# Turning copies with VectorE squares and DMAs in a two-layer hybrid encoder

## Chip, cores, metric

The kernel runs on one core of a Trainium2 chip. The metric is the device time of one execution in microseconds (us); smaller is better.

## What is computed

Two layers run over 256 tokens of width 2048, float32 in and out. Of the reference this matters:

```python
h = rmsnorm(x, pre_norm_g[l])
proj = jnp.einsum('bsd,dn->bsn', h, w_in[l])
(qa, ka, va, qb, kb, vb, qc, kc, vc, za, zb, zc, gates) = jnp.split(proj, ...)
ya = neighbourhood_attention(qa, ka, va, rpb[l])      # 8 heads
yb = gqa_attention(qb_h, kb_h, vb)                    # 8 heads, 2 of k and v; normed and rotated
yc = dilated_mixture(qc, kc, vc)                      # 3 groups of 4 heads, one softmax
g = sigmoid(gates + b_gate[l])
merged = (ga * ((ya * silu(za)) @ w_branch_a[l]) + gb * ((yb * silu(zb)) @ w_branch_b[l])
          + gc * ((yc * silu(zc)) @ w_branch_c[l]))
x = x + rmsnorm(merged @ w_out[l], post_norm_g[l])
```

Attention needs queries and keys with the head's 128 columns on the partitions, and its probabilities with the keys on the partitions; the projections by `w_branch` and `w_out` need their input with the columns on the partitions. A projection leaves the tokens on the partitions. So every such tensor is transposed once.

## The kernel before

**Weights.** All weights stream through the core once. A block is 512 output columns; its rows come in chunks of 256 (512 KB). A layer has 35 blocks of 8 chunks by the input weights, four times three smaller blocks by the branch weights (4, 2 and 4 chunks) and four blocks of 8 chunks by the output weight: 352 chunks a layer, 704 in all. SyncE (SP) issues one DMA a chunk into a tile `raw` (`emit_raw`, line 155; the first two chunks come by two DMAs each, line 163, all others by line 165). ScalarE rounds `raw` to a high part `wh` (line 171), VectorE subtracts it for the low part `wl` (line 176). TensorE multiplies each chunk for both token tiles T of 128 tokens, 12 matmuls of 512 columns a chunk (`mm3`, lines 146 to 148).

**Order.** The order of each engine's instructions is written out by the loop at line 737. Before chunk i it emits the `raw` up to chunk i+6, `wh` up to i+3 and `wl` up to i+2 (`ahead`, line 179; further in a few blocks), then the chunk's matmuls, then one `slot()` (line 100). A slot takes up to two steps of finished blocks' evacuations, one step of every active filler, and starts one new filler: first from `light` (transposes of evacuated blocks, put there by `later`), else from `heavy` (attention heads), no more than one head in 2 slots for the branches A and B, one in 4 for C. Every engine works through its own instructions in order; SP's queue holds the weight loads and all other DMAs.

**Buffers.** All large tiles come from one pool of 47 buffers of 4 KB a partition (`U`, line 59), taken in the order in which they come free. A DMA or an engine that writes into a buffer waits until its last reader is through.

**Transposes.** Everything that must be turned goes through TensorE as a 128x128 transpose into PSUM (`tp`), four side by side, and is copied or split from there into a high and a low part (`split`, line 128):

- `tr_job` (line 280): evacuated q, k, z and the rotated q, k of branch B, one job per token tile; transposes on line 284.
- `head_job` (line 360, branches A and B): a head's two products of scores, softmax, `norm`, then four transposes of the probabilities (line 380), a split, two slots later the products `o` with the values.
- `job_c` (line 407): the same for C, eight transposes a head through `four_T` (line 140).
- `mt_job` (line 568): the merged branches, through `four_T`.
- `ht_psum` (line 247): the second layer's input, through `four_T`; this one stays.

The split that follows is one ScalarE and one VectorE instruction. A head starts two slots after the one before it and takes nine slots in all; the heads of branch B start when the last tile of their q block has been evacuated.

Of the kernel before, what the change touches and what calls it, by code (L numbers as in the profile page):

```python
# [28 lines left out]
LAG = 6  # L29


class Blk:
    """One 512-column block of a projection: K chunks of 256 rows, both token tiles."""
# [14 lines left out]
def trunk(ctx, tc, x, xT, wpack, wbr_a, wbr_b, wbr_c, wout, pre_g, qk_g, bgate, post_g, abias,  # L48
# [32 lines left out]
    # the engines wake while the first loads are under way  # L81
# [11 lines left out]
    def later(g, wait=0):  # L93
        """a filler for a following slot, once what it needs is under way"""
        light.append((flow["slot"] + wait, g))
# [26 lines left out]
    def rsqrt(v, n):  # L122
        """1/sqrt of a small positive f32 tile"""
        y = small.tile([P, n], F32, name="rs_y")
        nc.gpsimd.tensor_tensor(out=y, in0=v, in1=mhalf[:, :n], op=ALU.pow)
        return y

    def split(src, h, lo, scale=1.0):
        """src * scale -> h + lo, both exactly representable for the one-pass products."""
# [6 lines left out]
    def four_T(src):  # L136
        """Four [128,128] transposes side by side in one bank."""
        tp = aux.tile([P, 4, P], F32, name="tp", bufs=2)
        for j in range(4):
            nc.tensor.transpose(tp[:, j, :], src(j), ident)  # L140
        return tp

    def mm3(out_, lhs, rhs, first, last):
        """out_ += lhs.T @ rhs for (high, low) pairs: one-pass products"""
# [60 lines left out]
    prev = {}  # L205

    def layer(l):
# [6 lines left out]
        # -- the layer's input: hT = (x * gain) transposed, 1/rms kept apart --  # L214
# [24 lines left out]
        def ht_x(nb, js):  # L239
            """from the host's transposed layout of x"""  # L240
# [6 lines left out]
        def ht_psum(nb, T):  # L247
            """from the previous layer's output: residual, transposes"""
# [30 lines left out]
        # -- evacuations, per token tile --  # L279
        def tr_job(dst, tok, T, n=4):  # L280
            """token-major [tok, n x 128] -> dst[column, block, tokens of T]; a pair is split"""
            tp = aux.tile([P, 4, P], F32, name="tp", bufs=2)
            for j in range(n):
                nc.tensor.transpose(tp[:, j, :], tok[:, T, j * P:(j + 1) * P], ident)  # L284
            c = slice(T * P, (T + 1) * P)
            if isinstance(dst, tuple):
                split(tp[:, 0:n], dst[0][:, 0:n, c], dst[1][:, 0:n, c])
            else:
                nc.scalar.copy(dst[:, 0:n, c], tp[:, 0:n])
            yield  # L290

        def evac_qk(store, key, which, two):
            tok = {}

            def f(T, ps):
# [4 lines left out]
                later(tr_job(store[key], tok[0], T))  # L300
# [16 lines left out]
        def evac_z(key):  # L317
            tok = {}

            def f(T, ps):  # L320
# [6 lines left out]
                later(tr_job(SZ[key], tok[0], T), 1)  # L327
# [3 lines left out]
        # -- attention --  # L331
        def softmax(sc, p, n, w, f=None):
            """n x w logits a row: exp(f * (s - max)), and the sums"""
# [11 lines left out]
        def norm(p, sm, n, rsh):  # L345
            """rows divided by their sums, times the gate's factor of the token"""
# [13 lines left out]
        def head_job(zb, hh, q, k, v, bias=None, f=None):  # L360
            """one head over all 256 keys, both token tiles: q, k give (high, low) of [d, tokens],
            v those of [keys of a tile, d]"""
# [14 lines left out]
            tp = aux.tile([P, 2, 256], F32, name="tp", bufs=2)  # L377
            for T in range(2):
                for kk in range(2):
                    nc.tensor.transpose(tp[:, kk, T * P:(T + 1) * P], p[:, T, kk * P:(kk + 1) * P], ident)  # L380
            pp = U("pp", [2, 2, 256], FR)
            ph, pl = pp[:, 0], pp[:, 1]
            split(tp, ph, pl)
# [23 lines left out]
        def job_c(hh, dist):  # L407
            """one merged head: the three groups' keys under one softmax"""
# [24 lines left out]
            px = U("px", [2, 256])  # L433
            for T in range(2):
                c = slice(T * P, (T + 1) * P)
                tp = four_T(lambda j: ps_[T][:, 0, j * P:(j + 1) * P])
                split(tp[:, 0:2], ph[:, :, c], pl[:, :, c])
                nc.scalar.copy(px[:, :, c], tp[:, 2:4])
                yield
# [10 lines left out]
        # -- branch A: two units of four heads --  # L450
# [17 lines left out]
        # -- branch B --  # L468
# [10 lines left out]
        def rope(dst, ps, T, n, which):  # L479
            """dst = rotation of ps (n heads), the norm's gain in the tables; in two steps"""  # L480
# [15 lines left out]
        def head_norm(ps, T, n):  # L496
            """1/rms of each head (of the normalised input's projection)"""
# [8 lines left out]
        def evac_qb(u):  # L506
            tok = {}

            def f(T, ps):
# [7 lines left out]
                later(tr_job(QT["b", u], tok[0], T), 1)  # L517
                if T == 1:
                    for hh in range(4):
                        heavy.append((2, job_b(u, hh)))  # L520
            return f

        def evac_kvb(T, ps):
# [14 lines left out]
            later(tr_job(KT["b"], tok, T, n=2), 1)  # L538
# [7 lines left out]
        # -- gates and branch products --  # L546
        def merge(nb):
# [20 lines left out]
            def mt_job(T):  # L568
                if nb not in MT:
                    MT[nb] = pair("mT", [4, 256])  # L570
                h, lo = MT[nb]
                c = slice(T * P, (T + 1) * P)
                tp = four_T(lambda j: G[0][:, T, j * P:(j + 1) * P])
                split(tp, h[:, :, c], lo[:, :, c], scale=0.5)
                yield

            def evac_p(i):
                def f(T, ps):
# [3 lines left out]
                    if i == 1:  # L582
                        later(mt_job(T))
# [9 lines left out]
        # -- output projection, post norm, residual --  # L593
# [258 lines left out]
```

## Time and profile before

| | |
|---|---|
| time, median of 3 runs (lowest to highest) | 2075.34 us (2074.78 to 2075.48) |
| span of the profiled execution, first to last instruction | 2073.5 us |
| around the span, against the median | 1.8 us |
| TensorE matmuls busy | 2061.9 us, 99% |
| VectorE, ScalarE busy | 1163.2 us (56%), 951.4 us (46%) |
| bytes moved by DMA | 397.81 MB, 192 GB/s |

The three runs lie within 0.04%. Busy time of TensorE includes matmuls that overlap one another: of two neighbours the next starts before the one before has ended, so the step from start to start is what a matmul costs. Instructions that only issue a DMA are listed under SPq and are not counted as busy time.

### The profile page before, as it was taken

What the parts mean: (1) busy time and instruction counts of PE and PEld (TensorE: products, weight loads), DVE (VectorE), ACT (ScalarE), POOL (GpSimd) and SP (SyncE); (2) the same over time, 40 slices, a digit from 0 to 9 for tenths busy, and PEclk for the clock granted to TensorE, in tenths of its full rate; (3) what the DMA queues carried; (4) which work ended last, traced back from release to release, by engine and by line L of the source; (5) the groups of instructions that cost most, each with busy time, mean ns of one, the idle gap of its engine ahead of it and who ended that gap; (6) DMA issues with size and microseconds to landing.
All of it is one profiled execution on the core that took longest, in us unless ns stands there. A gap on an engine that the chain in (4) does not pass through costs nothing.

```text
span 2073.5 us, 24944 instructions
## 1 busy us (share of the span) xinstructions
PE 2061.9 (99%) x9634; PEld 1716.2 (83%) x9634; DVE 1163.2 (56%) x1445; ACT 951.4 (46%) x1370; POOL 23.2 (1%) x31
## 2 busy tenths in 40 slices
PE   9999999999999999999999999999999999999998
PEld 7888888888888888888888888888888888888886
DVE  6444466565776554645554445565657764646454
ACT  6443354444554434443564444454445543443332
POOL 0000000000000000000000000000000000000000
PEclk9999999999999999999999999999999999999999
DMA  9555455645546655667565554555454466656662
GB/s 373 190 173 187 153 173 179 213 156 185 168 163 208 203 198 188 203 228 259 174 228 171 188 183 142 182 176 200 164 187 163 168 213 200 197 191 208 228 241 71
DMA packets 115270, 397.81 MB, mean 192 GB/s; under 512 B 12752, under 2 KB 12880, under 8 KB 115152
## 3 DMA queue, kind: packets, MB, share of 16 engines
q1 hardware_dynamic: 115152, 396.23, 56.5%
q8 instruction: 75, 1.23, 0.2%
q14 instruction: 43, 0.35, 0.1%
HBM read 391.99 MB, written 4.19 MB: 191 GB/s over the span
## 4 chain that ended last, share of the span: by engine, by line
PE 99%; DMA 0%; ACT 0%; DVE 0%; SPq 0%; issue 0%; DVEq 0%; POOLq 0%; ACTq 0%
PE acc L148 31%; PE acc L146 31%; PE acc L147 31%; PE tp L284 1%; PE tp L140 1%; PE tp L380 1%; PE o L148 0%; PE sc L148 0%; PE o L147 0%; PE sc L147 0%; PE o L146 0%; PE sc L146 0%; DMA raw<-in_wpack_dram 0%; PE o L446 0%; PE sc L418 0%; DVE x L597 0%
## 5 line engine op out<-in xcount | busy, mean ns | idle before, releaser
L176 DVE TENSOR_TENSOR wl<-raw,wh 128x1024 fp32r<-128x1024 f32 (+1 forms) x706 | 831.7, 1217 | 172.1 <-ACT wh L171 169.3
L146 PE MATMUL acc<-wh,hTh 128*128 128x512 f32 x2240 | 886.3, 396 | 0.6 <-ACT wh L171 0.6
L147 PE MATMUL acc<-wl,hTh 128*128 128x512 f32 x2240 | 873.8, 390 | 0.8 <-DVE wl L176 0.8
L148 PE MATMUL acc<-wh,hTl 128*128 128x512 f32 x2240 | 873.8, 390 | 0.0
L171 ACT CAST wh<-raw 128x1024 fp32r<-128x1024 f32 (+1 forms) x706 | 699.3, 1043 | 40.0 <-DVE wl L176 12.9
L148 PEld LDWEIGHTS acc<-wh,hTl 128*128 128x128 f32 x2240 | 420.6, 188 | 89.0
L147 PEld LDWEIGHTS acc<-wl,hTh 128*128 128x128 f32 x2240 | 421.5, 188 | 84.9 <-DVE wl L176 2.6
L146 PEld LDWEIGHTS acc<-wh,hTh 128*128 128x128 f32 x2240 | 421.2, 188 | 83.3 <-ACT wh L171 1.6
L564 ACT ACTIVATE g<-g 128x512 f32<-128x512 f32 x48 | 30.4, 633 | 232.8 <-DVE g L563 232.8
L563 DVE SCALAR_TENSOR_TENSOR g<-acc,rsx,bg 128x512 f32<-128x512 f32 x48 | 35.9, 747 | 173.6 <-PE acc L148 173.6
L146 PE MATMUL acc<-wh,yTh 128*128 128x512 f32 x320 | 124.5, 389 | 0.0
L147 PE MATMUL acc<-wl,yTh 128*128 128x512 f32 x320 | 124.5, 389 | 0.0
L148 PE MATMUL acc<-wh,yTl 128*128 128x512 f32 x320 | 124.5, 389 | 0.0
L146 PE MATMUL acc<-wh,mTh 128*128 128x512 f32 x256 | 100.4, 392 | 0.0
L148 PE MATMUL acc<-wh,mTl 128*128 128x512 f32 x256 | 99.7, 390 | 0.0
L147 PE MATMUL acc<-wl,mTh 128*128 128x512 f32 x256 | 99.7, 389 | 0.0
L299 ACT ACTIVATE tok<-acc,rsx 128x512 f32<-128x512 f32 x40 | 27.6, 689 | 124.9 <-PE acc L148 124.9
L340 ACT ACTIVATE sp<-sp,nm 128x256 f32<-128x256 f32 (+1 forms) x48 | 27.6, 577 | 109.4 <-DVE nm L335 109.4
L579 DVE SCALAR_TENSOR_TENSOR g<-g,acc 128x512 f32<-128x512 f32 x48 | 32.8, 683 | 78.6 <-PE acc L148 78.6
L147 PEld LDWEIGHTS acc<-wl,yTh 128*128 128x128 f32 x320 | 60.1, 188 | 12.5
L146 PEld LDWEIGHTS acc<-wh,yTh 128*128 128x128 f32 x320 | 60.1, 188 | 12.5
L130 ACT ACTIVATE mTh<-tp 128x512 fp32r<-128x512 f32 x16 | 9.6, 598 | 132.4 <-PE tp L140 132.4
(116 smaller groups left out, 1172.2 us busy)
## 6 DMA issues: line engine op xcount, KB each, us to landing
raw<-in_wpack_dram SPq DMA_DIRECT2D x558, 512.0 KB, 3.5
raw<-in_wo_dram SPq DMA_DIRECT2D x64, 512.0 KB, 5.2
raw<-in_wa_dram SPq DMA_DIRECT2D x32, 512.0 KB, 3.3
raw<-in_wb_dram SPq DMA_DIRECT2D x32, 512.0 KB, 3.7
raw<-in_wc_dram SPq DMA_DIRECT2D x16, 512.0 KB, 3.8
bg<-in_bgate_dram SPq DMA_DIRECT2D x24, 256.0 KB, 3.8
x<-in_x_dram SPq DMA_DIRECT2D x8, 512.0 KB, 7.9
abias<-in_abias_dram SPq DMA_DIRECT2D x8, 512.0 KB, 4.2
```

Of the source, the lines that this page charges most:

```text
L140: nc.tensor.transpose(tp[:, j, :], src(j), ident)
L146: nc.tensor.matmul(out_, lhsT=lh, rhs=rh, start=first, stop=False)
L147: nc.tensor.matmul(out_, lhsT=lh, rhs=rl, start=False, stop=False)
L148: nc.tensor.matmul(out_, lhsT=ll, rhs=rh, start=False, stop=last)
L171: nc.scalar.copy(HI[i][:, k], RAW[i][:, k])
L176: nc.vector.tensor_tensor(out=LO[i][:, k], in0=RAW[i][:, k], in1=f32(HI[i][:, k]), op=ALU.subtract)
L284: nc.tensor.transpose(tp[:, j, :], tok[:, T, j * P:(j + 1) * P], ident)
L299: nc.scalar.activation(tok[0][:, T], ps, AF.Copy, scale=S[which][T])
L340: nc.scalar.activation(p[:, i], sc[:, i], AF.Exp, bias=nm[:, i:i + 1], scale=1.0 if f is None else f[:, i:i + 1], accum_out=sm[:, i:i + 1])
L563: nc.vector.scalar_tensor_tensor(g, ps, S["rs"][T], BG[i], op0=ALU.mult, op1=ALU.add)
L564: nc.scalar.activation(g, g, AF.Tanh, scale=0.5)
L579: nc.vector.scalar_tensor_tensor(G[i][:, T], G[i][:, T], 1.0, ps, op0=ALU.add, op1=ALU.mult)
```

## The change

TensorE's transposes go, except those of `ht_psum`. In their place `turn` takes the two token tiles of a [128, n x 128] tensor; VectorE transposes each in 32x32 squares into a tile `tt` (one instruction per token tile), and 16 DMAs issued by SP carry the squares from row block i, column block j to row block j, column block i of a tile `tx`. Each DMA moves 32 partitions with one run of 2 x n x 32 numbers: 32 KB for n = 4, 16 KB for n = 2. `tt` and `tx` come from the pool of 47. Then three slots pass (`TR_WAIT`), and copy or split read `tx` (in SBUF) instead of `tp` (in PSUM).

- A block's two token tiles are turned together, once the second is evacuated.
- The heads of branch B are put into `heavy` by that job, when it is done.
- A head of A or B takes three slots more, and its split is made per token tile (2 x 256 columns where it was 512).
- The factor 0.5 of the merged branches is left out, and the norm behind them gets 4 * EPS instead, which cancels.

```diff
+TR_WAIT = 3
...
+    def turn(srcs, n):
+        tt, tx = U("tt", [4, 2, n * 32]), U("tx", [4, 2, n * 32])
+        for T in range(2):
+            nc.vector.transpose(out=tt[:, :, T].rearrange("p j (h a) -> p h j a", h=n), in_=srcs[T])
+        for i in range(4):
+            for j in range(4):
+                nc.sync.dma_start(out=tx[j * 32:(j + 1) * 32, i], in_=tt[i * 32:(i + 1) * 32, j])
+        return tx
...
-        def tr_job(dst, tok, T, n=4):
-            tp = aux.tile([P, 4, P], F32, name="tp", bufs=2)
-            for j in range(n):
-                nc.tensor.transpose(tp[:, j, :], tok[:, T, j * P:(j + 1) * P], ident)
-            c = slice(T * P, (T + 1) * P)
-            if isinstance(dst, tuple):
-                split(tp[:, 0:n], dst[0][:, 0:n, c], dst[1][:, 0:n, c])
-            else:
-                nc.scalar.copy(dst[:, 0:n, c], tp[:, 0:n])
-            yield
+        def tr_job(dst, tok, n=4, then=None):
+            tx = turn([tok[:, T] for T in range(2)], n)
+            for _ in range(TR_WAIT):
+                yield
+            for T in range(2):
+                src = turned(tx, T, n)
+                v = lambda t: squares(t[:, 0:n], T)
+                if isinstance(dst, tuple):
+                    split(src, v(dst[0]), v(dst[1]))
+                else:
+                    nc.scalar.copy(v(dst), src)
+            if then:
+                then()
...
-                later(tr_job(store[key], tok[0], T))
+                if T == 1:
+                    later(tr_job(store[key], tok[0]))
...
         def head_job(zb, hh, q, k, v, bias=None, f=None):
...
-            tp = aux.tile([P, 2, 256], F32, name="tp", bufs=2)
-            for T in range(2):
-                for kk in range(2):
-                    nc.tensor.transpose(tp[:, kk, T * P:(T + 1) * P], p[:, T, kk * P:(kk + 1) * P], ident)
+            tx = turn([p[:, T] for T in range(2)], 2)
+            for _ in range(TR_WAIT):
+                yield
             pp = U("pp", [2, 2, 256], FR)
             ph, pl = pp[:, 0], pp[:, 1]
-            split(tp, ph, pl)
+            for T in range(2):
+                split(turned(tx, T, 2), squares(ph, T), squares(pl, T))
...
         def job_c(hh, dist):
...
+            tx = turn([ps_[T][:, 0] for T in range(2)], 4)
+            for _ in range(TR_WAIT):
+                yield
             for T in range(2):
-                c = slice(T * P, (T + 1) * P)
-                tp = four_T(lambda j: ps_[T][:, 0, j * P:(j + 1) * P])
-                split(tp[:, 0:2], ph[:, :, c], pl[:, :, c])
-                nc.scalar.copy(px[:, :, c], tp[:, 2:4])
-                yield
+                src = turned(tx, T, 4)
+                split(src[:, 0:2], squares(ph, T), squares(pl, T))
+                nc.scalar.copy(squares(px, T), src[:, 2:4])
+            yield
+            yield
...
-                later(tr_job(QT["b", u], tok[0], T), 1)
                 if T == 1:
-                    for hh in range(4):
-                        heavy.append((2, job_b(u, hh)))
+                    later(tr_job(QT["b", u], tok[0],
+                                 then=lambda: heavy.extend((2, job_b(u, hh)) for hh in range(4))), 1)
...
-            def mt_job(T):
-                if nb not in MT:
-                    MT[nb] = pair("mT", [4, 256])
-                h, lo = MT[nb]
-                c = slice(T * P, (T + 1) * P)
-                tp = four_T(lambda j: G[0][:, T, j * P:(j + 1) * P])
-                split(tp, h[:, :, c], lo[:, :, c], scale=0.5)
-                yield
+            def mt_job():
+                MT[nb] = pair("mT", [4, 256])
+                return tr_job(MT[nb], G[0])
...
-                    nc.vector.tensor_scalar(v, v, 1.0 / DM, EPS, op0=ALU.mult, op1=ALU.add)
+                    nc.vector.tensor_scalar(v, v, 1.0 / DM, 4 * EPS, op0=ALU.mult, op1=ALU.add)
```

## Rows read from the trace of the kernel before

**Rows 1.** The page's part 1: span and busy time of each engine
```profile
span 2073.5 us, 24944 instructions
PE 2061.9 (99%) x9634; PEld 1716.2 (83%) x9634; DVE 1163.2 (56%) x1445; ACT 951.4 (46%) x1370; POOL 23.2 (1%) x31
```
**Rows 2.** Part 4 of the page: share of the chain that ended last, by engine
```profile
PE 99%; DMA 0%; ACT 0%; DVE 0%; SPq 0%; issue 0%; DVEq 0%; POOLq 0%; ACTq 0%
```
**Rows 3.** Groups of instructions by form: the transposes (busy us, mean ns | idle before)
```profile
L284 PE MATMUL tp<-ident,tok 128*128 128x128 f32 x280 | 42.2, 272 | 0.0
...
L380 PE MATMUL tp<-ident,sp 128*128 128x128 f32 x128 | 19.1, 272 | 0.0
...
L140 PE MATMUL tp<-ident,sp 128*128 128x128 f32 x64 | 9.6, 272 | 0.0
...
L140 PE MATMUL tp<-ident,g 128*128 128x128 f32 x64 | 9.6, 272 | 0.0
```
**Rows 4.** Chain that ended last, 542 to 624 us: start us, us on the chain
```profile
558.79 0.44 PE tp L380 x4
...
560.16 0.23 PE acc L147
```
**Rows 5.** SP's timeline: two pairs of issues with nothing between (start us, us)
```profile
1.65 0.90 SPq L163 DMA_DIRECT2D raw<-in_wpack_dram  x2
...
461.00 0.81 SPq L165 DMA_DIRECT2D raw<-in_wpack_dram  x2
```
**Rows 6.** Line 165, whole span: one issue, ns min/median/max
```profile
L165 SPq DMA_DIRECT2D raw<-in_wpack_dram x558: 327/328/1693, 4.5 to 1916.3; - x186
```
**Rows 7.** SP's waits: total us, times, longest us
```profile
SPq L165 <- PE acc L148: 734.6, 254, 7.1
```
**Rows 8.** Line 165 and one product's group, 0 to 540 us: how many by then
```profile
L165 SPq DMA_DIRECT2D raw<-in_wpack_dram x187: 327/328/1693, 4.5 to 539.8; - x187
...
L148 PE MATMUL acc<-wh,hTl 128*128 128x512 f32 x712 | 277.8, 390 | 0.0
```
**Rows 9.** Busy time by stretch, line 140 alone, then 380, then 284: PE, PEld, PEclk
```profile
247.50:323.50 76.00, 4.78 (x32) 3.99 (x32) 1.00 0.53 178
...
351.50:398.50 47.00, 2.39 (x16) 1.89 (x16) 1.00 0.59 202
449.00:499.00 50.00, 2.39 (x16) 1.89 (x16) 1.00 0.59 195
542.00:622.00 80.00, 4.79 (x32) 3.77 (x32) 1.00 0.47 160
...
247.50:323.50 76.00, 3.59 (x24) 2.85 (x24) 1.00 0.53 178
351.50:398.50 47.00, 2.40 (x16) 1.97 (x16) 1.00 0.59 202
449.00:499.00 50.00, 2.39 (x16) 1.97 (x16) 1.00 0.59 195
542.00:622.00 80.00, 2.40 (x16) 1.95 (x16) 1.00 0.47 160
```
**Rows 10.** Groups of instructions by form: the casts and the nearest VectorE operations
```profile
L176 DVE TENSOR_TENSOR wl<-raw,wh 128x1024 fp32r<-128x1024 f32 x702 | 829.1, 1220 | 171.6 <-ACT wh L171 168.9 <-DMA raw<-in_wpack_dram 2.6
L171 ACT CAST wh<-raw 128x1024 fp32r<-128x1024 f32 x702 | 696.9, 1045 | 39.5 <-DVE wl L176 12.9 <-PE acc L147 12.4 <-DMA raw<-in_wpack_dram 7.2
...
L493 DVE TENSOR_TENSOR tok<-tok,s 128x512 f32<-128x512 f32 x8 | 5.5, 692 | 0.3
L493 DVE TENSOR_TENSOR tok<-tok,s 128x256 f32<-128x256 f32 x4 | 1.7, 425 | 0.1
```
**Rows 11.** The DMA view: bytes; issues by line, KB each, median us to landing
```profile
DMA packets 115270, 397.81 MB, mean 192 GB/s; under 512 B 12752, under 2 KB 12880, under 8 KB 115152
...
raw<-in_wpack_dram SPq DMA_DIRECT2D x558, 512.0 KB, 3.5
...
gpre<-in_pre_g_dram SPq DMA_DIRECT2D x1, 16.0 KB, 1.8
```

More of the change, by code (lines that the diff above doesn't have):

```diff
@@ L141, in four_T, with turned, squares @@
         return tp
+    def turn(srcs, n):
[6 more added lines that the diff above has]
+        return tx
+    def turned(tx, T, n):
+        return tx[:, :, T].rearrange("p i (h a) -> p h i a", h=n)
+    def squares(t, T):
+        return t[:, :, T * P:(T + 1) * P].rearrange("p h (i a) -> p h i a", i=4)
     def mm3(out_, lhs, rhs, first, last):
@@ L326, in f @@
                 nc.vector.scalar_tensor_tensor(z, z, 1.0, ps, op0=ALU.add, op1=ALU.mult)
-                later(tr_job(SZ[key], tok[0], T), 1)
+                if T == 1:
+                    later(tr_job(SZ[key], tok[0]), 1)
                 yield
@@ L537, in evac_kvb @@
                 nc.scalar.activation(t, t, AF.Copy, scale=f[:, i:i + 1])
-            later(tr_job(KT["b"], tok, T, n=2), 1)
+            if T == 1:
+                later(tr_job(KT["b"], tok, n=2), 1)
         def go_c():
@@ L581, in f @@
                         nc.vector.tensor_tensor(out=G[0][:, T], in0=G[0][:, T], in1=G[i][:, T], op=ALU.add)
-                    if i == 1:
-                        later(mt_job(T))
+                    if i == 1 and T == 1:
+                        later(mt_job())
                     yield
```

## Prediction

> **What bounds the kernel now.** The first view is the page's summary of engines: TensorE's matmuls are busy for 99% of the span, VectorE 56%, ScalarE 46% [rows 1]. Busy time alone would not prove a bound; the chain of waits does: it is TensorE's own for 99% [rows 2]. So whatever leaves TensorE's queue is gained in full, as long as everything that TensorE waits for still comes in time. One chunk is 12 matmuls; a product's piece of the chain is 0.23 us [rows 4], so a slot is 2.75 us of TensorE time, and 704 of them make 1936 of the 2073.5 us.
>
> The second thing to see is SP's queue. It is no engine of the busy table, but it feeds every chunk. Two issues with nothing between them take 0.81 to 0.90 us [rows 5], so one DMA costs SP about **0.43 us**, of which the issue proper is 0.33 [rows 6]. Today SP spends 0.43 of each 2.75 us on issuing and waits for the rest, mostly for a buffer that TensorE has yet to free [rows 7]. It runs far ahead: by 540 us it has issued 187 loads of line 165 after the two chunks of line 163, 189 in all, while TensorE has done 3 x 712 / 12 = 178 chunks [rows 8]. That lead of 11 chunks is what the change spends.
>
> **What is removed.** The groups of transposes [rows 3] hold 280 + 128 + 64 + 64 = 536. The chain shows four of them in 0.44 us [rows 4], 0.11 each, though a single one is listed with 272 ns (they overlap). All stand in TensorE's queue on the path: 536 x 0.111 = **59.5 us gained**. The Trainium skill, page "VectorE: DVE Perf Modes", section "The three transpose paths", gives 390 ns for a 128x128 TensorE transpose. By that figure the gain would be an estimated 209 us; the trace has the duration for the same thing, so the 0.111 stands.
>
> **What is added.** Turns per layer: 10 blocks of q and k, 5 of z, one of k and two of q in branch B, 4 merged blocks, 20 heads: 42, so 84 turns, 168 VectorE transposes and **1344 DMAs**, all on SP.
>
> - VectorE squares: the trace has none. Nearest are VectorE operations from SBUF to SBUF on as many elements: 0.69 us for 512 columns, 0.43 for 256; the difference, 0.27 for 256 columns, gives 0.53 for 512 if nothing is fixed, and twice the columns take 1.22 [rows 10]. I take 0.69 and 0.43, the nearest in form. With 50 turns of n = 4 and 34 of n = 2 this is 100 x 0.69 + 68 x 0.43 = 98 us: VectorE rises from 1163 to some 1260 us, 61%. It does not become the bound.
> - Copies and splits: same work from SBUF; the 32 heads of A and B split in two halves instead of one, at most one operation of 256 columns more each, 32 x 0.43 = 14 us. Hidden under the idle 40% of ScalarE and VectorE; were that cover gone, 14 us in all.
> - Bytes: 50 x 524 KB + 34 x 262 KB = 35 MB against 398 [rows 11], 9% more. The DMA engines are busy for about half of each stretch below (the second last column of rows 9), so they have room.
> - SP: one turn is 16 x 0.43 = **6.9 us** of its queue, 2.5 slots. Behind a turn's DMAs are queued the weight loads that follow in the written order, and the turn's first DMA waits for the squares, which wait on VectorE behind `wl`. So SP, far ahead until now, is pulled back to TensorE's place at each turn: the written order lets a load lead by 6 chunks, the 6.9 us take 2.5 of them, landing (3.5 us [rows 11]) another 1.3. `wh` is cast 3 chunks ahead. One turn by itself uses the lead up, no more; I cost it at **nothing**. From its first square to the last landing it takes 1.4 + 6.9 + 1.8 to 3.5 (a 16 KB and a 512 KB DMA [rows 11]) = 10 to 12 us against three slots, 8.25 us; the weights cast 2 to 3 chunks ahead cover the difference. If that cover is gone, each such turn costs 2 to 4 us; there are 13 a layer outside the stretches below.
>
> **Where turns come close together.** Four stretches of a layer hold the heads. The counts of transposes by line and stretch [rows 9] give the turns (8 per block, 4 per head of A and B, 8 per head of C), and what is left to TensorE when they go:
>
> - C, 76 us: 4 heads, 3 blocks, 7 turns, 56 transposes (6.2 us): 69.8 us.
> - A first, 47 us: 4 heads, 2 blocks, 6 turns, 3.6 us: 43.4.
> - A second, 50 us: the same counts, 46.4.
> - B, 80 us: 8 heads, 2 blocks, 10 turns, 5.3 us: 74.7.
>
> Seven to ten us a turn, then. What does SP need a turn? Once the lead is used up, work is in series: a load issued behind the last turn (0.43), its cast (1.05), its subtraction (1.22) [rows 10], two squares in VectorE's order behind it (1.38 or 0.86), 16 DMAs (6.9): 10.98 us for n = 4, 10.46 for n = 2. I count the load's landing as covered, since a load issued one turn earlier is there. The stretches then take: C 7 x 10.98 = 76.9; A 4 x 10.46 + 2 x 10.98 = 63.8 each; B 8 x 10.46 + 2 x 10.98 = 105.6. The losses are 7.1 + 20.4 + 17.4 + 30.9 = 75.8 us a layer, **151.6 in two layers**.
>
> Bounds. From below, 16 issues of 0.33 and the three loads between turns at 0.33 are 6.3 us a turn; that is less than what TensorE has to do in every stretch, and the loss is nothing. From above, the landing of 3.5 us is in series too: 14.5 and 14.0 us, stretches of 101.5, 85 twice and 141, losses of 31.7 + 41.6 + 38.6 + 66.3 = 178 a layer, 356 in all. I take the middle way because the nearest rows (the pairs of issues, the casts) carry it and a lead of one load remains.
>
> **Sum.** 2073.5 - 59.5 + 151.6 = 2165.6 us of span; with the 1.8 us around it **2167 us**, 4.4% slower than the median of 2075.34. Start, layer boundary and tail hold no turn on the path. At a layer's end the last merged block is needed by the seventh chunk of the output product, 6 x 2.75 = 16.5 us after its start; it is ready after two slots, the turn's 10 to 12 us and a split of 0.7, so 16 to 18 us: 0 to 2 us a layer, taken as nothing.
>
> **Rivals.**
>
> 1. *The transfers stay hidden.* The small DMAs (32 rows instead of 128) are issued faster than loads, or the lead of 11 chunks carries each stretch. For it: SP is idle for most of the span, and the sum of its issues, with the 704 loads, (1344 + 704) x 0.43 = 881 us, is 42% of it. Against: rows 5 and 6 show the same issue time for loads of different size, and the stretches are short of time, not the span. Result 2075.3 - 59.5 = **2016 us**. It decides where a turn takes less than 8.8 us: then 22 x 8.8 - 164.5 (A and B) = 29.7 a layer, half the gain; that is 0.11 us less per DMA, 0.32. The Trainium skill, page "DMA: Bandwidth & Descriptors", section "Issuing engines are not separate DMA queues", calls the time to initiate a DMA "usually small relative to the DMA itself", and by that rule this rival holds. The rows here: 0.33 us of issue beside 1.8 us to landing for 16 KB, so small for one, not for 16 in a row.
> 2. *Gain and loss cancel.* A turn at 8.8 us: **2075 us**.
> 3. *The landing is in series too*, because the pool of 47 buffers has two more per turn to give and each load waits for a buffer that a turn's DMAs still read: **2372 us**, or anything above 2260.
> 4. *TensorE's clock falls.* The granted clock is 1.00, so 2.4 GHz, in all stretches [rows 9], where TensorE never stops. The stalls forecast here are of several us. Nothing in the trace bounds this; if 20 stalls were each followed by 5 us at 1.2 GHz, some 50 us more: **2217 us**.
>
> **Chances.** The forecast 0.66, its own range 2090 to 2260. Rival 1 0.17 (a third of that with a little loss, 2050 to 2070). Rival 2 0.06, of which 0.04 lie within 0.2%, about what a measurement of this kernel can tell from no change, and 0.01 on each side. Rival 3 0.08. Rival 4 0.03. Faster: 0.17 + 0.01 = 0.18; same 0.04; slower 0.66 + 0.01 + 0.08 + 0.03 = 0.78. The range of 2050 to 2260 leaves out the clean case of rival 1 (0.12) and rival 3 (0.08).
>
> **What the profile after would show.** Transposes of lines 284 and 380 gone, about 32 left on line 140; 1344 new issues on SP at 0.4 us or so, 16 in 6 to 7 us. In the chain of waits TensorE's share falls below 97% and SP, VectorE's `wl` and the new DMAs appear. Idle time of TensorE before `acc` is released by `wl` or `wh`, and stands in the stretches of heads, B most (some 30 us a layer), not in the first blocks nor in the gate blocks of the later merges, where each block should be 0.9 us shorter per turn. SP's lead falls from 11 to about 6 chunks there. I am wrong if SP's issues are well under 0.3 us, if TensorE stays at 99%, or if its idle time stands at every turn, also at the lonely ones.

## The result, and the profile after

The changed kernel takes **2365.9 us** (median of four, 2359.6 to 2368.3) beside 2075.1 us for the kernel before on the same chip: ratio 1.140, 95% interval 1.138 to 1.141. It is slower, as predicted, but by 291 us instead of 92, and outside the range of 2050 to 2260 us.

The page of the kernel after: span and engines (part 1), the granted clock by slice (part 2), the chain's shares by engine (part 4), two kinds of DMA (part 6: KB each, median us to landing).

```profile
span 2366.3 us, 26208 instructions
...
PE 2131.2 (90%) x9098; PEld 1723.2 (73%) x9098; DVE 1249.8 (53%) x1645; ACT 979.6 (41%) x1402; POOL 21.2 (1%) x31
...
PEclk9999989898978999999999999998989889999999
...
PE 40%; SPq 17%; DMA 7%; DVE 4%; issue 3%; ACT 2%; ACTq 0%; DVEq 0%; POOLq 0%
...
raw<-in_wpack_dram SPq DMA_DIRECT2D x558, 512.0 KB, 6.8
...
tx<-tt SPq DMA_DIRECT2D x800, 32.0 KB, 1.9
...
tx<-tt SPq DMA_DIRECT2D x544, 16.0 KB, 1.8
```

Against [rows 1, 2]: 536 matmul instructions are gone, TensorE stands idle for 10% of the span, the chain is no longer its own, and SP has come into it with 17%. A weight load lands 6.8 us after its issue instead of 3.5 [rows 11].

The new lines 152 (the 16 DMAs) and 149 (the squares), each with ns min/median/max:

```profile
L152 SPq DMA_DIRECT2D tx<-tt x1344: 507/588/1771, 51.1 to 2281.9; - x192
...
L149 DVE STREAM_TRANSPOSE tt<-sp x80: 400/436/706, 250.6 to 1927.9; 128x256 f32<-128x256 f32 x64, 128x512 f32<-128x512 f32 x16
L149 DVE STREAM_TRANSPOSE tt<-tok x72: 401/672/709, 49.8 to 1841.7; 128x512 f32<-128x512 f32 x68, 128x256 f32<-128x256 f32 x4
```

An issue is 0.588 us, where a load's is 0.328 [rows 6]. SP's timeline in the first layer's stretch of branch B, start us and us; an entry is a run of issues of one kind:

```profile
663.68 10.74 SPq L152 DMA_DIRECT2D tx<-tt  x16
674.46 0.58 SPq L580 DMA_DIRECT2D bg<-in_bgate_dram  x1
675.14 0.85 SPq L183 DMA_DIRECT2D raw<-in_wpack_dram  x2
676.10 21.73 SPq L152 DMA_DIRECT2D tx<-tt  x32
697.93 1.95 SPq L183 DMA_DIRECT2D raw<-in_wpack_dram  x4
704.56 10.01 SPq L152 DMA_DIRECT2D tx<-tt  x16
714.61 1.05 SPq L183 DMA_DIRECT2D raw<-in_wpack_dram  x2
715.80 11.40 SPq L152 DMA_DIRECT2D tx<-tt  x16
...
764.37 10.76 SPq L152 DMA_DIRECT2D tx<-tt  x16
775.23 1.95 SPq L183 DMA_DIRECT2D raw<-in_wa_dram  x4
```

This is the loss of that stretch in one view. Sixteen issues take 10.0 us when nothing holds them, 0.63 apiece with the gap between; the longer entries hold waits of under 1 us. Nine turns go by from 663.68 to 775.13, 12.4 us each, and between the entries SP stands still only once, 4.7 us before 704.56. Weight loads get through two or four at a time. TensorE needs some 7.5 us for what lies between two turns (74.7 us for ten, in the prediction), so it starves. What it waits for, over the whole span (total us, times, longest us):

```profile
PE o L164 <- ACT pp L131: 79.4, 30, 5.2
PE acc L165 <- DVE wl L194: 74.8, 56, 5.9
PE acc L164 <- ACT wh L189: 30.2, 15, 5.7
```

The casts of the weights (`wl` and `wh`) hold it for 105 us, as the prediction has it; the products `o` with the values wait nearly as long for the copies of turned probabilities (`pp`), which the prediction has not. Waits on ScalarE, VectorE and SP, in the same way:

```profile
DVE wl L194 <- ACT wh L189: 244.6, 116, 11.3
ACT pp L131 <- DMA tx<-tt: 228.3, 40, 10.4
...
ACT wh L189 <- DMA raw<-in_wpack_dram: 181.5, 198, 5.9
...
SPq L152 <- DVE tt L149: 407.5, 39, 20.6
SPq L183 <- PE acc L166: 309.8, 124, 7.0
```

Copies wait for the turn's DMAs, casts for the weights, and SP for the squares. SP's wait for buffers that TensorE frees has fallen from 734.6 us [rows 7] to 309.8. Its lead, counted as in the prediction, is 2, 1 and 1 chunks at 400, 540 and 740 us, inside the heads' stretches, where the prediction expected about 6: it is used up. The busy time of four stretches (from:to, us, then PE, PEld, DVE, ACT, POOL busy, granted clock, DMA share, GB/s):

```profile
294.00:332.00 38.00, 30.33 (x119) 22.97 (x118) 19.44 (x32) 15.44 (x25) 0.00 (x0) 0.87 0.53 186
...
394.00:435.00 41.00, 32.21 (x120) 24.64 (x119) 19.60 (x34) 11.76 (x20) 0.00 (x0) 0.83 0.34 114
...
685.00:737.00 52.00, 33.12 (x140) 26.81 (x139) 24.14 (x53) 17.53 (x35) 0.00 (x0) 0.77 0.36 111
737.00:784.00 47.00, 34.29 (x123) 26.29 (x122) 20.63 (x35) 15.97 (x25) 0.00 (x0) 0.82 0.43 149
```

The clock, 1.00 in all stretches before [rows 9], is granted at 0.77 to 0.87 here.

### The profile page after: what moved, and what is told of

It reads as the page before. It is cut to its first block, busy times and chain, and to the rows that moved or that the text cites. A ratio compares the mean times of both kernels' runs of the same rounds, so it can differ in the third digit from the quotient of the medians.

```text
span 2366.3 us, 26208 instructions
## 1 busy us (share of the span) xinstructions
PE 2131.2 (90%) x9098; PEld 1723.2 (73%) x9098; DVE 1249.8 (53%) x1645; ACT 979.6 (41%) x1402; POOL 21.2 (1%) x31
## 4 chain that ended last, share of the span: by engine, by line
PE 40%; SPq 17%; DMA 7%; DVE 4%; issue 3%; ACT 2%; ACTq 0%; DVEq 0%; POOLq 0%
SPq L152 16%; PE acc L165 13%; PE acc L166 13%; PE acc L164 13%; DMA raw<-in_wpack_dram 5%; DVE wl L194 2%; ACT wh L189 1%; DMA tx<-tt 1%; SPq L183 1%; DMA raw<-in_wo_dram 1%; DVE tt L149 1%; SPq L580 0%; DVE g L602 0%; DVE s L518 0%; DVE tok L520 0%
## 5 line engine op out<-in xcount | busy, mean ns | idle before, releaser
L165 PE MATMUL acc<-wl,hTh 128*128 128x512 f32 x2240 | 908.9, 406 | 73.8 <-DVE wl L194 73.3
L164 PE MATMUL acc<-wh,hTh 128*128 128x512 f32 x2240 | 905.8, 404 | 28.9 <-ACT wh L189 28.7
L166 PE MATMUL acc<-wh,hTl 128*128 128x512 f32 x2240 | 897.8, 401 | 0.0
L189 ACT CAST wh<-raw 128x1024 fp32r<-128x1024 f32 (+1 forms) x706 | 716.3, 1045 | 287.3 <-DMA raw<-in_wpack_dram 181.5
L164 PEld LDWEIGHTS acc<-wh,hTh 128*128 128x128 f32 x2240 | 438.9, 196 | 127.6 <-ACT wh L189 36.2
L166 PEld LDWEIGHTS acc<-wh,hTl 128*128 128x128 f32 x2240 | 437.3, 195 | 91.6
L133 DVE TENSOR_TENSOR pp<-tx,pp 128x256 fp32r<-128x256 f32 x80 | 31.2, 423 | 213.2 <-ACT pp L131 207.0
L131 ACT ACTIVATE pp<-tx 128x256 fp32r<-128x256 f32 x80 | 29.8, 410 | 228.3 <-DMA tx<-tt 228.3
L133 DVE TENSOR_TENSOR qkl<-tx,qkh 128x512 fp32r<-128x512 f32 x32 | 20.7, 688 | 149.4 <-ACT qkh L131 139.3
L590 DVE SCALAR_TENSOR_TENSOR g<-acc,rsx,bg 128x512 f32<-128x512 f32 x48 | 35.9, 747 | 110.4 <-PE acc L166 110.4
L131 ACT ACTIVATE qkh<-tx 128x512 fp32r<-128x512 f32 x32 | 18.4, 623 | 151.5 <-DMA tx<-tt 129.5
L602 DVE SCALAR_TENSOR_TENSOR g<-g,acc 128x512 f32<-128x512 f32 x48 | 32.9, 685 | 72.8 <-PE acc L166 72.8
```

The costliest lines, as they stand in the source:

```text
L131: nc.scalar.activation(h, src, AF.Copy, scale=scale)
L133: nc.vector.tensor_tensor(out=lo, in0=src, in1=f32(h), op=ALU.subtract)
L164: nc.tensor.matmul(out_, lhsT=lh, rhs=rh, start=first, stop=False)
L165: nc.tensor.matmul(out_, lhsT=lh, rhs=rl, start=False, stop=False)
L166: nc.tensor.matmul(out_, lhsT=ll, rhs=rh, start=False, stop=last)
L189: nc.scalar.copy(HI[i][:, k], RAW[i][:, k])
```

## The experiments

Theories: **Q**, SP's queue is too short of time for a turn's issues; **W**, the pause of three slots is too short for a turn; **S**, the loss follows the issues to whichever queue issues them. Each run is set beside runs of the kernel before on its chip (2075.1 to 2075.4 us).

### Four and eight issues a turn

First four, then eight:

```diff
-            for j in range(4):
-                nc.sync.dma_start(out=tx[j * 32:(j + 1) * 32, i], in_=tt[i * 32:(i + 1) * 32, j])
+            nc.sync.dma_start(out=tx[:, i], in_=tt[:, i])
```

```diff
-            for j in range(4):
-                nc.sync.dma_start(out=tx[j * 32:(j + 1) * 32, i], in_=tt[i * 32:(i + 1) * 32, j])
+            for k in range(2):
+                nc.sync.dma_start(out=tx[k * 64:(k + 1) * 64, i], in_=tt[k * 64:(k + 1) * 64, i])
```

Both leave out the move of the squares to another row block; they price the issues.

> Each turn is carried by 4 DMAs of 128 partitions instead of 16 of 32; the bytes, the two buffers, the squares and the waits stay. The squares stay in their own row block, so this part of the transposition is left out. Theory Q (SP's queue: a turn costs 16 issues of 0.63 us, 10.1 us, and in the heads' stretches work runs in series behind them): a turn costs SP 4 x 0.43 to 0.63 = 1.7 to 2.5 us, less than any stretch needs, so the loss goes and the 59.5 us of transposes are gained: 2016 to 2040 us, granted clock 1.00. Theory B (two more buffers a turn starve the loads) and theory D (bytes): nothing they need has changed, so above 2250 us. If the 32 rows make an issue dear, these cost 0.43 us each; if the way from SBUF to SBUF does, 0.63.

> Eight DMAs of 64 partitions a turn instead of 16 of 32; the squares stay in their own row blocks, so this part of the transposition is left out. Between the change (16 issues, 2366 us) and four issues (2016 us) theory Q gives a curve: 8 x 0.63 = 5.1 us and in series with load, casts and squares 9.2 us for n = 4, 8.7 for n = 2. C 64 us against 69.8, no loss; A 53.2 against 43.4 and 46.4, 9.8 and 6.8; B 88 against 74.7, 13.3; 30 us a layer: 2016 + 60 = 2076 us. If the cost lay in the shape of 32 rows and not in the number, the time would be that of four issues, 2016 us, with issues under 0.5 us.

Measured: **2016.4 us** with four (0.972 [0.970, 0.973]) and **2047.8 us** with eight (0.987 [0.985, 0.988]). With the same squares, copies, buffers and bytes the change brings its full 59.5 us when a turn is four issues. So neither buffers nor bytes cost anything. The kernel with four, page parts 1 and 6 and its issues:

```profile
span 2014.6 us, 24913 instructions
...
PE 2000.1 (99%) x9098; PEld 1660.6 (82%) x9098; DVE 1247.4 (62%) x1645; ACT 968.4 (48%) x1402; POOL 24.4 (1%) x31
...
raw<-in_wpack_dram SPq DMA_DIRECT2D x558, 512.0 KB, 6.4
...
L151 SPq DMA_DIRECT2D tx<-tt x336: 465/593/2186, 51.3 to 1926.0; - x168
```

The weight loads land late here too, 6.4 us after their issue, and SP stands for the squares for 561.5 us; neither costs anything. Each issue is 0.593 us, though of 128 rows and four times the bytes: the price goes with the number of issues, not with rows or bytes. Eight came out 28 us better than expected.

### A longer pause

```diff
-TR_WAIT = 3
+TR_WAIT = 6
...
-                return tr_job(MT[nb], G[0])
+                return tr_job(MT[nb], G[0], wait=3)
```

> Six slots instead of three between the turn and the copies (three for the merged branches). Theory Q: SP's queue is as full as before, so within 40 us of 2366 us, on either side. Theory W (a turn of 1.4 + 10.1 + 1.9 = 13.4 us against three slots of 8.25 us: ScalarE and VectorE stand still in the copies, and only this is late): six slots, 16.5 us, cover it, and most of the loss goes: 2016 to 2120 us.

Measured: **2379.7 us** (1.147 [1.145, 1.149]). W falls: with twice the pause nothing is gained.

### Half of the turns

```diff
+            tp = aux.tile([P, 2, 256], F32, name="tp", bufs=2)
+            for T in range(2):
+                for kk in range(2):
+                    nc.tensor.transpose(tp[:, kk, T * P:(T + 1) * P], p[:, T, kk * P:(kk + 1) * P], ident)
```

These lines stand for the whole edit: the heads' turns, or the blocks' and merged branches', or all but 13, go back to TensorE as in the kernel before.

> The heads' probabilities go back to TensorE, blocks and merged branches are turned as in the change: 44 turns, 344 transposes fewer than before, 38 us. Theory Q: the stretches hold 3, 2, 2 and 2 turns in 76, 47, 50 and 80 us, some 25 us for each against 14.2 us in series, so nothing is lost there: 2037 us, up to 2055 if each merged block keeps the 2 us it loses now. Theory W: every turn is 5 us late, 44 x 5 = 220 us: about 2257 us.

> Blocks and merged branches go back to TensorE, the heads' probabilities are turned as in the change: 40 turns, 192 transposes fewer than before, 21 us. Theory Q: the stretch C has 4 turns of 14.2 us in 76 us, no loss; A 4 of 13.7 us = 54.8 against 45.2 and 48.2 us, 9.6 and 6.6; B 8 of 13.7 = 109.6 against 76.4, 33.2; 49 us a layer, 99 in two, 2075 - 21 + 99 = 2153 us. Theory W: 40 turns 5 us late each, 2254 us, with the loss in C like that in A and B.

> Only the turns of the first stage stay (q and k of branch C in both layers, z of C in the second): 13 turns, 104 transposes of TensorE fewer than before; all else goes through TensorE again. The blocks concerned took 21.8 us in the change against 22.7 before. Theory Q: turns 22 us apart cost nothing, 11.5 us are gained: 2064 us. Theory W: each turn is 5 us late: 2129 us.

Measured: **2154.5 us** (1.038) with the 44 turns of blocks and merged branches alone, **2221.3 us** (1.070) with the 40 of the heads, **2071.2 us** (0.998 [0.997, 0.999]) with the 13 lonely ones. The first two met neither theory. The 344 transposes that the first of them (e3) takes from TensorE give 38 us, so 2037 us were to be had: it lost 117 us, 2.7 per turn. Counted by the ends of the blocks' last matmuls, some 40 us of that stand at the 26 turns outside the heads' stretches, about 1.5 each. So a lone turn does not cost nothing at 10 us a turn. The heads alone lost 167 us (2221 less 2075 and the 21 of 192 transposes), 4.2 per turn; both together the change loses 350. The 13 turns gained 4 of the 11.5 us that they should. Their expectation took the blocks concerned to last 21.8 us in the change; most did, but the second q block took 30.3.

### Other queues

```diff
-                nc.sync.dma_start(out=tx[j * 32:(j + 1) * 32, i], in_=tt[i * 32:(i + 1) * 32, j])
+                eng = nc.sync if j % 2 == 0 else nc.scalar
+                eng.dma_start(out=tx[j * 32:(j + 1) * 32, i], in_=tt[i * 32:(i + 1) * 32, j])
```

> Eight of a turn's 16 DMAs are issued by ScalarE's queue, eight by SP's; all is computed. Theory Q: SP spends 5.1 us a turn as with eight DMAs, 2076 us, if ScalarE (41% busy) bears 84 x 8 x 0.63 = 423 us of issuing. Rival S: ScalarE stands in its own order behind the squares as SP did, and its casts wait: the loss only moves, above 2200 us.

Measured: **2219.1 us** (1.069 [1.068, 1.071]). Half of the added time goes with half of the issues, the rest turns up in ScalarE's own order, where casts stand behind its issues, as S has it (waits as above):

```profile
ACT wh L190 <- DMA tx<-tt: 610.8, 77, 26.7
```

### Through HBM in five issues

One store of `tt`, and a slot later four loads that pick all squares of a row block.

```diff
+        nc.sync.dma_start(out=d, in_=tt.rearrange("p j t f -> p j (t f)"))
+        return d, n
+    def carry(dn):
...
+        for j in range(4):
+            nc.sync.dma_start(out=tx[j * 32:(j + 1) * 32].rearrange("p i t f -> p i (t f)"),
+                              in_=d[:, j].rearrange("(i r) f -> r i f", i=4))
```

> A turn goes through HBM: one DMA stores the squares as they are (128 rows), in the next slot four DMAs load them back by row block of the destination: 5 issues instead of 16, 70 MB more traffic; all is computed. Theory Q: 5 issues cost SP 2.2 to 3.2 us a turn, in series 6.3 to 7.3 us, under or at what the stretches need: 2016 to 2040 us, faster than both. Rival W (only the way to the copies is too long): squares 1.4, store 2.8, four issues and a landing 5 us, 9 us and more against three slots of 8.25, like the change with its 13.4; then above 2100 us.

Measured: **2068.2 us** (0.996 [0.995, 0.998]): more bytes, two trips, and 298 us less than the change. Its issues, ns min/median/max:

```profile
L153 SPq DMA_DIRECT2D scr_dram<-tt x84: 319/327/432, 53.1 to 1968.6; - x84
...
L160 SPq DMA_DIRECT2D tx<-scr_dram x336: 302/424/1472, 56.3 to 1973.8; - x168
```

0.33 and 0.42 us against 0.59 between two tiles of SBUF. With HBM on one side the 0.43 with the gap, which the prediction took from [rows 5], nearly holds: a load of this kind takes 0.47 us with the gap behind it, a store 0.38 to 0.39.

Four more steps on it: merged branches on TensorE (e9), a pause of four slots (e10), the turns' DMAs on GpSimd (e11), loads two slots behind the store and a pause of five (e15). The edit from e9 to e15:

```diff
-TR_WAIT = 3
+TR_WAIT = 5
...
-                if k == 0:
+                if k == 1:
                     tx = carry(tx)
```

> The kernel of e7 (one store to HBM and four loads back per turn), with the eight merged branches' turns given back to TensorE. In e7 what was lost against the full gain of 59.5 us is 2068 - 2016 = 52 us; of it some 2 us stand at each merged branch and 6.5 us at each layer's first block of the output product. Theory Q (the price of a turn on SP's queue; a turn that something waits for soon is late): 64 transposes come back, 7 us, and 2 x 6.5 + 6 x 2 = 25 us go: about 2050 us. If the merged turns are late for a reason that is not the turn (the gate's own operations), the blocks stay as long and it is 2068 + 7 = 2075 us.

> The kernel of e9 with a pause of four slots instead of three between a turn's squares and their use. Theory W (what is left in e9 is the time from the squares to the landing of the second trip, some 9 to 10 us, against three slots of 2.75 us): the copies no longer hold ScalarE and VectorE, about 2030 us. Theory Q (what is left is SP standing for the store of a turn before it may issue the loads behind it): the same as e9 within 5 us.

> The kernel of e10 with the store and the four loads of each turn issued on GpSimd's queue instead of SP's; SP then issues weight loads alone, as in the kernel before. Theory Q: what was lost by SP standing behind the squares and the stores is gained, 2020 to 2035 us, near the 2023 us of a kernel that loses nothing (2016 and the 7 us of the merged branches). Rival: GpSimd's issues are dearer or later than SP's, so the copies wait for the landing instead and the loss stays: 2045 us or more, with the wait of ScalarE's copies for the turn's landing longer than in e10.

> The kernel of e10 (store to HBM, four loads back, merged branches on TensorE) with the loads back one slot later (two slots behind the store instead of one) and a pause of five slots instead of four. Theory: what is left in e10, 16 us above the 2023 us of a kernel that loses nothing, is SP standing for the store of a turn (172 us in 76 waits) with weight loads queued behind; with another slot the store has landed: 2025 to 2033 us. Rival: the store is late because its squares are, so SP stands for the squares whatever the pause, and the longer way to a head's output adds at the last head of each stretch: 2039 us or a little more.

Measured: e9 **2049.2**, e10 **2039.1**, e11 **2174.1** (1.046 [1.043, 1.049]), e15 **2026.9 us** (0.977 [0.975, 0.978]). e9 came as Q has it, e10 between its theories. SP's wait for the store, first in e10, then in e15:

```profile
SPq L160 <- DMA scr_dram<-tt: 172.2, 76, 6.3
```
```profile
SPq L160 <- DMA scr_dram<-tt: 83.2, 58, 3.8
```

One more slot halves that wait, and the time falls by 12 us, as the theory has it; the pause grew with it, so the two are not told apart. e11's rival came true: GpSimd stands in its own order for the squares, and ScalarE's copies wait for the turns' landing, `pp` for 118.5 us where e10 has 20.0.

```profile
POOL scr_dram L153 <- DVE tt L149: 409.5, 32, 70.4
...
ACT pp L131 <- DMA tx<-scr_dram: 118.5, 25, 9.3
```

Its loads also land 5.2 instead of 3.0 us after their issue (128 KB, the DMA views of the two runs). Which of these takes how much of the 135 us between e11 and e10 is not known.

The first three merged branches turned by VectorE again:

```diff
-                        later(mt_job())
+                        later(mt_job() if nb == 3 else mt_turned())
```

> The kernel of e15 (store, four loads two slots later, pause of five slots) with the first three merged branches of each layer turned by VectorE again and only the last, which the output product needs at once, on TensorE: 48 transposes fewer, 48 x 0.111 = 5.3 us. Theory: with five slots a merged turn holds nobody, 2021 to 2022 us. Rival: the merged turns of e7 cost some 2 us each for another reason (ScalarE's gate operations behind the copy): 6 x 2 - 5 = 7 us more than e15, 2034 us.

Measured: **2021.5 us** (0.974 [0.973, 0.976]), the best version that does all the work, faster than both kernels: 54 of the 59.5 us.

### Is it the price of an issue alone?

```diff
-            for i in range(4):
-                nc.sync.dma_start(out=tx[j * 32:(j + 1) * 32].rearrange("p i t f -> p i (t f)"),
-                              in_=d[:, j].rearrange("(i r) f -> r i f", i=4))
+            for i in range(4):
+                nc.sync.dma_start(out=tx[j * 32:(j + 1) * 32, i].rearrange("p t f -> p (t f)"),
+                                  in_=d[i * 32:(i + 1) * 32, j])
```

> The kernel of e7 with sixteen loads of 32 rows instead of four of 32 rows and four times the width: 17 issues a turn, all of them between HBM and SBUF. The issues from HBM were seen at 0.33 to 0.43 us against 0.59 to 0.63 between two tiles of SBUF, so a turn takes 17 x 0.40 to 0.43 = 6.8 to 7.3 us of SP's queue, about the 6.9 that the prediction had. Theory P (the prediction's sum holds, the price of an issue alone was mis-sized): near the predicted 2167 us, 2130 to 2220 with the second trip's landing and the lone turns. Theory N (the number of issues decides, whatever they cost): as the changed kernel or slower, 2366 us or more. If issues of SP behind each other cost little here, it stays near e7's 2068.

Measured: **2360.8 us** (1.137 [1.136, 1.139]). It can't decide, since the store's trip got into SP's queue. SP's timeline, as above:

```profile
712.96 8.21 SPq L161 DMA_DIRECT2D tx<-scr_dram  x16
721.27 0.37 SPq L193 DMA_DIRECT2D raw<-in_wpack_dram  x1
721.73 0.38 SPq L153 DMA_DIRECT2D scr_dram<-tt  x1
722.16 0.42 SPq L193 DMA_DIRECT2D raw<-in_wpack_dram  x1
725.85 7.54 SPq L161 DMA_DIRECT2D tx<-scr_dram  x16
```

Sixteen issues take 8 instead of 10 us, but SP stands for 3.3 us (722.58 to 725.85): 12.9 us from turn to turn, where the change has 12.4, and nearly the same time. So it seems that how long a turn holds SP counts, whether it issues or stands. The next pair shortens just that (eleven; for thirteen the numbers are 2, 1, 0, 0):

```diff
-        for i in range(4):
-            for j in range(4):
+        for i, wide in enumerate((2, 2, 1, 0)):
+            for k in range(wide):
+                nc.sync.dma_start(out=tx[k * 64:(k + 1) * 64, i], in_=tt[k * 64:(k + 1) * 64, i])
+            for j in range(2 * wide, 4):
                 nc.sync.dma_start(out=tx[j * 32:(j + 1) * 32, i], in_=tt[i * 32:(i + 1) * 32, j])
```

> The changed kernel with 11 DMAs a turn instead of 16: five of them carry 64 rows each, six 32, all between two tiles of SBUF, the same bytes (the squares that the wide ones carry are not moved among the partitions, so the probabilities and copies are turned in part only; nothing else is left out). 11 x 0.633 us = 6.96 us a turn on SP: the turn of the prediction, 6.9 us, by fewer and dearer issues. Theory P (the prediction's sum holds and the price of an issue alone was mis-sized): 2167 us, 2145 to 2190. Theory M (more is missing in the sum, as the turns that stand alone, or the clock): clearly above, 2200 us or more. Rival (the series of load, cast, subtraction and squares that the sum puts beside the issues is hidden for the most part): under 2120 us.

> The same with 13 DMAs a turn (three of 64 rows, ten of 32; the wide ones again without the move of squares). 13 x 0.633 = 8.23 us a turn. By the prediction's sum with that price a turn in series takes 12.3 (n = 4) or 11.8 us (n = 2); the stretches lose 16.3 + 28.4 + 25.4 + 44.3 = 114 us a layer, 229 in two, less 59.5: theory P 2244 us, 2220 to 2270. Theory M: 2290 or more. Rival (the series is hidden for the most part): under 2200 us.

Measured: **2137.7 us** (1.030 [1.029, 1.032]) and **2220.2 us** (1.070 [1.068, 1.072]): between P and the rival that hides the series, at the edge of P for 13. At the predicted turn of 6.9 us the sum is 29 us too high. SP's timeline with eleven, line 152 the wide ones:

```profile
642.27 3.06 SPq L152 DMA_DIRECT2D tx<-tt  x5
645.37 3.76 SPq L154 DMA_DIRECT2D tx<-tt  x6
649.17 1.33 SPq L185 DMA_DIRECT2D raw<-in_wpack_dram  x2
650.68 3.06 SPq L152 DMA_DIRECT2D tx<-tt  x5
653.78 4.32 SPq L154 DMA_DIRECT2D tx<-tt  x6
658.20 0.99 SPq L185 DMA_DIRECT2D raw<-in_wpack_dram  x2
659.30 3.06 SPq L152 DMA_DIRECT2D tx<-tt  x5
```

Turns start 8.4 and 8.6 us apart (9.0 on average over the six from 614.40 on): the issues, two loads, and under 0.3 us more. The sum had 10.46.

### The clock

```diff
+        if b.busy and T == 0:
+            for _ in range(3):
+                four_T(lambda j: ident)
```

> The changed kernel with twelve transposes of the identity, 3 x 0.44 = 1.3 us of TensorE work that nobody reads, put ahead of each chunk's matmuls in the nine blocks of a layer that have become longest (144 chunks in both layers, 190 us of TensorE work into idle time of some 280 us). TensorE's granted clock should rise in these blocks. Theory C (the lower clock is a part of the loss): the time falls below the changed kernel's 2366 us, down to 2300 to 2350. Theory N (SP's queue sets the pace of these blocks, so that a slower TensorE between its waits costs nothing): 2366 us within 10, although the clock rises. If the added work falls where TensorE does not wait, the time grows by up to 190 us, and the run says nothing of the clock.

Measured: **2394.9 us** (1.154 [1.152, 1.155]). 190 us of added TensorE work cost 29 us. Stretches of this kernel that answer to the first two above (columns as there):

```profile
294.00:330.00 36.00, 36.00 (x224) 31.59 (x223) 18.93 (x31) 14.18 (x23) 0.00 (x0) 1.00 0.55 191
...
399.00:439.00 40.00, 36.18 (x214) 30.72 (x213) 19.58 (x34) 11.84 (x20) 0.00 (x0) 1.00 0.35 116
```

The clock is back at 1.00 in these two, from 0.87 and 0.83, and in one more of the nine stretches of the first layer; in the other six it is 0.85 to 0.96. The first two blocks take 35.9 and 40.4 us where the change's take 38.3 and 41.4; most others grew, by up to 9 us. In the first TensorE is now busy for all 36.00 us, so it can set the pace itself, and the stretch says nothing of the clock's price. In the second SP's runs of issues fill nearly all the time in both kernels, and at a clock of 1.00 the block is 1 us shorter, of 17 lost: there theory N holds.

For the whole kernel a bound can be read from the pages. The change and the kernel with four issues have the same 9098 matmuls; TensorE is busy for 2131.2 us in the one and 2000.1 in the other. So of the 352 us between their spans 221 are idle time of TensorE, and 131 are longer busy time, at a mean granted clock of 0.944 against 0.999. The lower clock can have cost up to these 131 us. It came with the waits for SP's queue, since with four issues it stays at 0.999; how much of it would have been idle time otherwise stays open.

## Why the prediction was right in sign and wrong in size

Time by number of issues a turn: 2016 us with 4, 2048 with 8, 2138 with 11, 2220 with 13, 2366 with 16. A turn short enough costs nothing, as the prediction said. There is no sharp threshold: an issue more costs 8 us between 4 and 8, then 30, 41 and 49 us, towards the 53 us that 84 issues of 0.63 take.

- **The step that failed: "one DMA costs SP about 0.43 us".** It was read from loads, HBM to SBUF [rows 5, 6], and used for DMAs between two tiles of SBUF, of which there was no row. Such an issue costs 0.63. With 10.1 us a turn in place of 6.9 the prediction's own sum is 14.2 (n = 4) and 13.7 us (n = 2) a turn; the stretches lose 29.6 + 39.8 + 36.8 + 63.3 = 169.5 us a layer, 339 in all, and the result is 2355 us. No bound priced an issue that high: the lower bound had it cheaper by 0.1, the upper bound added a landing, none an issue dearer than any row.
- **How well the corrected sum fits.** Loss of each stretch against the kernel with four issues, mean of the two layers, counted from the ends of the blocks' last matmuls (blocks 12 to 14, 15 to 18, 19 to 22 and 23 to 26 of a layer):

| us a layer | C | A first | A second | B |
|---|---|---|---|---|
| prediction's sum, 6.9 us a turn | 7.1 | 20.4 | 17.4 | 30.9 |
| eleven issues, measured | 6.9 | 11.8 | 12.2 | 28.0 |
| the same sum, 10.1 us a turn | 29.6 | 39.8 | 36.8 | 63.3 |
| the change, measured | 30.1 | 32.9 | 30.4 | 63.8 |

C and B come out within 3 us at both prices. In both stretches of A together the sum is 13 to 14 us a layer too high; why is not known. With 16 issues some 38 us outside the stretches, which the sum has at nothing, make up for that, so the close 2355 is in part luck.

- **The series of load, cast, subtraction and squares** (3.6 us for n = 2): in part hidden. From 663.68 to 775.13 SP's runs of issues fill 95% of the time; a turn takes 12.4 us, not 13.7, and with eleven issues 9.0, not 10.46. That B's loss still is the sum's is then in part luck too; what else stands in B was not taken apart.
- **Place**: right in the main. Of the 352 us between the two spans 314 lie in the heads' stretches, B most, and 38 in the first blocks, the merged ones and the output product.
- **"A lone turn costs nothing"**: right at the predicted length: with eleven issues the blocks before the heads all take the 21.8 us of a block without transposes. At 10 us it fails: the second q block of the first layer rose from 23.7 to 30.3 us, and the 26 lone turns cost the 38 us above, 1.5 each, under the bound of 2 to 4. So one of the prediction's own signs of being wrong, idle time at the lonely turns, came in part.
- **The gain** of 59.5 us: right; with four issues, which leave the squares in their row blocks, 2016 us were measured, rival 1's figure. The 390 ns that the prediction quotes from the Trainium skill, page "VectorE: DVE Perf Modes", section "The three transpose paths", stand there for bf16; the transposes here are float32.
- **Squares, bytes**: right. 0.67 to 0.69 and 0.44 us a square operation against 0.69 and 0.43; VectorE 1250 us against 1260; 433 MB against 397.81 + 35. The copies and splits stay hidden: the kernel with four issues has them all and loses nothing.
- **Rivals.** Rival 3's time (2372) was nearly met, though not by its cause: the kernel with four issues takes the same buffers, its loads land nearly as late, and it loses nothing. Rival 1's condition, under 8.8 us a turn, was not met (its 29.7 us a layer should read 29.1; nothing else hangs on it). The Trainium skill, page "DMA: Bandwidth & Descriptors", section "Issuing engines are not separate DMA queues", calls the time to initiate a DMA usually small relative to the DMA itself; here 0.59 us of issue stand beside 1.8 us to landing, and sixteen hold the queue for 10. Rival 4 was right that the clock falls; what it costs is open, at most the 131 us above.

## What to carry to other kernels

Price an issue by the kind of transfer, and where no row of that kind exists, put the bound above the dearest row, not at it. Then count issues per turn, and what stands in series with them, against the work of the busiest engine between two turns: well below it they are free, well above it an extra issue is paid nearly in full. Here fewer, wider DMAs won even with more bytes and a second trip, and more so once the second trip's issues and the copies were put later.

## What the runs showed of the hardware that was not expected

- A DMA between two tiles of SBUF took 0.59 us to issue on SP, the same for 32, 64 and 128 rows; a store to HBM 0.33 and a load with small pieces 0.42. On GpSimd the same stores and loads took 0.56 and 0.55 us.
- TensorE's granted clock went down to 0.77 in a stretch where it was busy for 33 of 52 us, and it was at 1.00 in three of the nine stretches of a layer where work that nobody reads was put into the waits, 0.85 to 0.96 in the others.
